# First three gate and up strips of an FFN summed tile by tile of x, with x loaded on a second DMA queue

## The chip, the cores and the metric

The kernel runs on one core of a Trainium2 chip. The metric is device time in microseconds (us) from one launch to its end. The kernel before was timed in three runs: 2579.68, 2580.84 and 2581.11 us, median 2580.84. Beside the timed runs there is one profiled execution, whose trace all rows below come from.

## What is computed

One decoder layer on 320 tokens (256 of a prompt, 64 of eight samples), model width 2048, feed-forward width 5632. The part that the change touches is the first feed-forward block and the norm ahead of it:

```python
def rmsnorm(x, g):
    y = xf * lax.rsqrt(jnp.mean(xf * xf, axis=-1, keepdims=True) + EPS)
    return (y * g.astype(jnp.float32)).astype(x.dtype)

def swiglu_ffn(x, wg, wu, wd):
    return (jax.nn.silu(x @ wg) * (x @ wu)) @ wd

def block(x, ...):
    x = x + FFN_RES * swiglu_ffn(rmsnorm(x, n_f1), f1_g, f1_u, f1_d)
    m, s_new, b_new = mixer(rmsnorm(x, n_mix), ...)
    x = x + m
    x = x + cross_attn(rmsnorm(x, n_xa), mk, mv, xa_q, xa_o)
    x = x + FFN_RES * swiglu_ffn(rmsnorm(x, n_f2), f2_g, f2_u, f2_d)
```

All of it is in float32.

## The kernel before, in words

The activations lie transposed: the model width is cut into 16 tiles of 128 rows (KT = 16), and each tile xs[k] holds 320 tokens as columns. A product of a 128x128 weight block with such a tile is written as three matmuls (mm3, lines 173 to 179): weights and activations are each split in a rounded high part and the rest, and high·high, high·low and low·high are summed in PSUM. Lines 176, 177 and 178 are these three, in this order.

Weights come in units of 128x1024 float32 (512 KB), that is eight 128x128 blocks. fetch (line 126) loads one into a raw buffer (three of them) from SP's DMA queue, ACT casts the high part (line 116) and DVE subtracts the low part (line 117), into four pairs of buffers. unit (line 137) keeps the fetches up to four units ahead of their use. A unit feeds 8 products, 24 matmuls.

ffn (line 232) computes the hidden width in parts of eight strips of 128. For each strip, strip (line 181) sums the gate over all 16 tiles of x into one PSUM accumulator, and then the up projection into the next; there are four such accumulators (tag acc, line 89) and four small ones (tag sm, line 92). The norm is applied behind the product: DVE multiplies the gate's sum by r, the reciprocal root mean square (line 242), ACT applies SiLU (243), DVE multiplies by r again (244) and by the up sum (249), and the result is split into high and low. The down products of the part follow, 16 tiles of eight products each.

r of the first block is made by first_root (line 269), which is called behind the first gate strip: ACT squares each x tile, POOL adds the squares up (line 212), a matmul with a matrix of ones sums over the partitions (219), and root (line 189) forms the power -1/2 by Ln, Exp and a Newton step: two table loads, four ACT instructions, two DVE instructions (lines 192 to 197).

At the start (lines 320 to 326) SP's queue is given: vec (the constants with the norms' gains), x tile 0, the first weight unit, x tiles 1 to 3 and 4 to 7, the second unit, x tiles 8 to 11 and 12 to 15; scaled_split (line 226) multiplies each tile by its gain from vec and splits it on ACT (228) and DVE (229). setup (line 275) holds small work on vec (lines 292 to 301) that is not needed before the mixer.

Every instruction stream is in order on its engine. The order in each stream is drawn up when the program is built: an instruction is taken by its priority, which is its place in the source unless the source raises it (as fetch does), among those that are ready by the builder's own reckoning.

Of the kernel before, what the change touches and what calls it, by code (L numbers as in the profile page):

```python
# [17 lines left out]
P = 128  # L18
# [16 lines left out]
MEM = 256  # L35
EPS = 1e-6
# [26 lines left out]
def hymba(tc, A, O):  # L63
# [15 lines left out]
    with (  # L79
# [15 lines left out]
        xgrp = [cp.tile([P, 4, T], F32, name=f"x{g}") for g in range(4)]  # L95
        xs = [xgrp[k // 4][:, k % 4, :] for k in range(KT)]
# [29 lines left out]
        def fetch(early=False):  # L126
            with contextlib.nullcontext() if early else tc.high_priority():
                raw = tl(mp, [P, 1024], F32, "raw", 3)
                g, u = divmod(fetched[0], 2)
                nc.sync.dma_start(raw, A["w"][g, :, u * 1024 : (u + 1) * 1024])  # L130
                hi = tl(mp, [P, 1024], F32R, "whi", 4)
                lo = tl(mp, [P, 1024], F32R, "wlo", 4)
                split(hi, lo, raw)
                units.append((hi, lo))
            fetched[0] += 1
# [52 lines left out]
        # r = (ps / n + eps) ** -0.5, the tables' value and one step of Newton's  # L188
# [37 lines left out]
        def scaled_split(k, name):  # L226
            h, l = pair("xg")
            nc.scalar.activation(h, xs[k], AF.Copy, scale=norm(name, k))  # L228
            nc.vector.scalar_tensor_tensor(l, xs[k], norm(name, k), h.bitcast(F32), ALU.mult, ALU.subtract)  # L229
            return h, l  # L230

        def ffn(pool, xg, root_of, done, setup=None):
            for pi, np_ in enumerate(PARTS):
                last_part = pi == len(PARTS) - 1
                hs = []
                for _ in range(np_):
                    pg = acc()
                    strip(xg, pg[:, :T])
                    if pi == 0 and not hs:
                        r = root_of()  # L240
                    t = tl(pool, [P, T], F32, "fa", 2)
                    nc.vector.tensor_tensor(t, pg[:, :T], r, ALU.mult)  # L242
                    nc.scalar.activation(t, t, AF.Silu)  # L243
                    nc.vector.tensor_tensor(t, t, r, ALU.mult)  # L244
                    pu = acc()
                    strip(xg, pu[:, :T])
                    hp = pair("h")
                    h = tl(pool, [P, T], F32, "fb", 2)
                    nc.vector.tensor_tensor(h, pu[:, :T], t, ALU.mult)  # L249
                    split(*hp, h)  # L250
                    hs.append(hp)
# [12 lines left out]

        # first FFN
# [3 lines left out]
        def first_root():  # L269
            stat = Stat()  # L270
            for k in range(KT):
                stat.add(xs[k])
            return stat.rstd()

        def setup(fp):
# [27 lines left out]
            # the memory's root mean square  # L303
# [31 lines left out]
            # a projection of the prompt's memory, tokens on the partitions  # L335
# [327 lines left out]
        # cross attention  # L663
# [151 lines left out]
        # second FFN  # L815
        with phase("ffn2") as fp:
# [11 lines left out]
            for k0, k1 in ((0, 1), (1, 4), (4, 8), (8, 12), (12, 16)):  # L828
                y = xgrp[k0 // 4][:, k0 % 4 : k0 % 4 + k1 - k0, :]
                nc.vector.tensor_tensor(y, y, r.unsqueeze(1).to_broadcast([P, k1 - k0, T]), ALU.mult)  # L830
                nc.sync.dma_start(O["y"][:, k0:k1, :], y)
# [20 lines left out]
def ffn_groups(w_gate, w_up, w_down):  # L852
    g, u, d = strips(w_gate), strips(w_up), downs(w_down)
    out = []
    f0 = 0
    for pi, np_ in enumerate(PARTS):
        for j in range(f0, f0 + np_):
            out += [g[j : j + 1], u[j : j + 1]]
        out.append(d[pi])
        f0 += np_  # L860
# [3 lines left out]
def pack(i):  # L864
    f = {k: np.asarray(v) for k, v in i.items()}
    groups = ffn_groups(f["ffn1_w_gate"][0], f["ffn1_w_up"][0], f["ffn1_w_down"][0])
# [20 lines left out]
    x = np.ascontiguousarray(x.T.reshape(KT, P, T).transpose(1, 0, 2))  # L887
# [90 lines left out]
```

## Time and profile before

| what | value |
|---|---|
| median of three runs | 2580.84 us (2579.68 to 2581.11) |
| span of the profiled execution | 2581.1 us |
| matmul instructions | 17280 |
| TensorE (PE) busy, share of the span | 2538.0 us, 98% |
| VectorE (DVE) busy | 1473.7 us, 57% |
| ScalarE (ACT) busy | 1076.9 us, 42% |
| GpSimd (POOL) busy | 100.1 us, 4% |
| bytes moved by DMA | 397.37 MB, mean 154 GB/s |

The profiled execution's span differs from the median by 0.3 us. PE is TensorE's matmuls, PEld its weight loads; SPq and ACTq are the sequencers of SyncE and ScalarE, which issue DMAs. A busy time is summed over instructions that can overlap in the pipeline, so what the matmuls cost is read from the distance between starts.

### The profile page before, as it was taken

How to read it: one execution, taken by the hardware profiler on the slowest of the kernel's cores; microseconds unless marked ns; L12 is line 12 of the kernel's file. 1: busy time of each engine (PE TensorE's matmuls, PEld its weight loads, DVE VectorE, ACT ScalarE, POOL GpSimd, SP SyncE). 2: the span in 40 equal slices, each digit the busy share in tenths (PEclk: the TensorE clock that was granted, in tenths of full speed). 3: DMA queues.
4: the chain of work that ended last, by engine and by line, in shares of the span. 5: the costliest groups of instructions: out<-in, count | busy, mean ns of one | idle time of the engine just before them, and what ended most of it. 6: DMA issues, size and time to landing. Idle time of an engine off the chain costs nothing.

```text
span 2581.1 us, 41685 instructions
## 1 busy us (share of the span) xinstructions
PE 2538.0 (98%) x17280; PEld 2491.3 (97%) x17280; DVE 1473.7 (57%) x2110; ACT 1076.9 (42%) x1487; POOL 100.1 (4%) x105
## 2 busy tenths in 40 slices
PE   7999999999999999999999999999999999999997
PEld 7999999999999989999998898999999999999997
DVE  6544444444444478788878775744444444444444
ACT  6333333333233354565655744532333333333334
POOL 4000000000000020000000020200000000000002
PEclk9999999999999999999999999999999999999999
DMA  7444444444444465444444554444444444444443
GB/s 234 156 151 150 148 150 152 148 150 152 148 149 153 148 195 160 146 156 141 150 144 146 198 176 150 147 152 148 150 152 148 150 152 148 150 153 148 150 152 107
DMA packets 111790, 397.37 MB, mean 154 GB/s; under 512 B 12656, under 2 KB 16368, under 8 KB 111600
## 3 DMA queue, kind: packets, MB, share of 16 engines
q1 hardware_dynamic: 111600, 394.70, 48.1%
q8 instruction: 136, 2.23, 0.3%
q14 instruction: 54, 0.44, 0.0%
HBM read 384.90 MB, written 9.76 MB: 153 GB/s over the span
## 4 chain that ended last, share of the span: by engine, by line
PE 92%; DVE 4%; ACT 2%; issue 1%; DMA 0%; POOL 0%; DVEq 0%; ACTq 0%; POOLq 0%
PE acc L176 29%; PE acc L177 29%; PE acc L178 29%; DVE wlo L117 1%; PE sm L512 1%; PE sm L605 1%; ACT whi L116 0%; DVE xgl L229 0%; DVE t L343 0%; PE sm L571 0%; ACT L194 0%; DVE hl L117 0%; ACT t L549 0%; DVE x L811 0%; PE sm L616 0%
## 5 line engine op out<-in xcount | busy, mean ns | idle before, releaser
L116 ACT CAST whi<-raw 128x1024 fp32r<-128x1024 f32 x688 | 721.7, 1049 | 1369.4 <-PE acc L177 983.7
L117 DVE TENSOR_TENSOR wlo<-raw,whi 128x1024 fp32r<-128x1024 f32 x688 | 849.6, 1235 | 557.2 <-ACT whi L116 556.7
L176 PE MATMUL acc<-xgh,whi 128*128 128x320 f32 x3648 | 1140.5, 313 | 11.5 <-ACT whi L116 9.4
L177 PE MATMUL acc<-xgl,whi 128*128 128x320 f32 x3648 | 1130.6, 310 | 3.5 <-DVE xgl L117 1.9
L178 PE MATMUL acc<-xgh,wlo 128*128 128x320 f32 x3648 | 1129.7, 310 | 1.8 <-DVE wlo L117 1.8
L176 PEld LDWEIGHTS acc<-xgh,whi 128*128 128x128 f32 x3648 | 686.8, 188 | 17.2 <-ACT whi L116 9.4
L177 PEld LDWEIGHTS acc<-xgl,whi 128*128 128x128 f32 x3648 | 687.2, 188 | 7.0 <-DVE xgl L229 3.2
L178 PEld LDWEIGHTS acc<-xgh,wlo 128*128 128x128 f32 x3648 | 686.7, 188 | 2.5 <-DVE wlo L117 2.5
L176 PE MATMUL acc<-hh,whi 128*128 128x320 f32 x1728 | 534.3, 310 | 2.4 <-DVE x L658 1.5
L178 PE MATMUL acc<-hh,wlo 128*128 128x320 f32 x1728 | 534.5, 309 | 0.0
L177 PE MATMUL acc<-hl,whi 128*128 128x320 f32 x1728 | 533.9, 309 | 0.0
L176 PEld LDWEIGHTS acc<-hh,whi 128*128 128x128 f32 x1728 | 324.1, 188 | 4.6 <-issue 3.0
L177 PEld LDWEIGHTS acc<-hl,whi 128*128 128x128 f32 x1728 | 324.3, 188 | 0.3 <-issue 0.2
L178 PEld LDWEIGHTS acc<-hh,wlo 128*128 128x128 f32 x1728 | 324.3, 188 | 0.2
L259 DVE SCALAR_TENSOR_TENSOR x<-acc,x 128x320 f32<-128x320 f32 x192 | 94.0, 491 | 223.0 <-PE acc L178 222.9
L212 POOL TENSOR_TENSOR ssq<-ssq,sq 128x320 f32<-128x320 f32 x74 | 83.8, 1133 | 1925.2 <-ACT sq L210 1021.0
L411 DVE SCALAR_TENSOR_TENSOR hl<-u,vec,hl 128x256 f32<-128x256 f32 x240 | 115.4, 481 | 2.3
L249 DVE TENSOR_TENSOR fb<-acc,fa 128x320 f32<-128x320 f32 x88 | 43.3, 492 | 111.0 <-PE acc L178 110.9
L242 DVE TENSOR_TENSOR fa<-acc,r 128x320 f32<-128x320 f32 x88 | 43.2, 492 | 109.1 <-PE acc L178 109.0
L229 DVE SCALAR_TENSOR_TENSOR xgl<-x,vec,xgh 128x320 fp32r<-128x320 f32 x48 | 47.3, 1016 | 0.9 <-ACT xgh L228 0.9
L117 DVE TENSOR_TENSOR hl<-fb,hh 128x320 fp32r<-128x320 f32 x88 | 43.2, 491 | 0.0
L244 DVE TENSOR_TENSOR fa<-fa,r 128x320 f32<-128x320 f32 x88 | 42.6, 485 | 0.6 <-ACT fa L243 0.6
(198 smaller groups left out, 1029.7 us busy)
## 6 DMA issues: line engine op xcount, KB each, us to landing
raw<-in_w SPq DMA_DIRECT2D x688, 512.0 KB, 3.8
t<-in_mem SPq DMA_DIRECT2D x8, 512.0 KB, 5.9
t<-in_s SPq DMA_DIRECT2D x8, 512.0 KB, 4.9
out_ss<-t SPq DMA_DIRECT2D x8, 512.0 KB, 3.6
kv<-in_ck SPq DMA_DIRECT2D x8, 512.0 KB, 6.3
kv<-in_cv SPq DMA_DIRECT2D x8, 512.0 KB, 6.2
t4k<-in_mem SPq DMA_DIRECT2D x4, 512.0 KB, 5.0
x<-in_x SPq DMA_DIRECT2D x3, 640.0 KB, 6.9
```

The lines of the kernel that those rows point to most:

```text
L116: nc.scalar.copy(hi, src)
L117: nc.vector.tensor_tensor(lo, src, hi.bitcast(F32), ALU.subtract)
L176: nc.tensor.matmul(out, hi, xh, start=first, stop=False)
L177: nc.tensor.matmul(out, hi, xl, start=False, stop=False)
L178: nc.tensor.matmul(out, lo, xh, start=False, stop=last)
L212: nc.gpsimd.tensor_tensor(self.total, self.total, s, ALU.add)
L229: nc.vector.scalar_tensor_tensor(l, xs[k], norm(name, k), h.bitcast(F32), ALU.mult, ALU.subtract)
L242: nc.vector.tensor_tensor(t, pg[:, :T], r, ALU.mult)
L244: nc.vector.tensor_tensor(t, t, r, ALU.mult)
L249: nc.vector.tensor_tensor(h, pu[:, :T], t, ALU.mult)
L259: nc.vector.scalar_tensor_tensor(xs[n], ps[:, :T], 0.5, xs[n], ALU.mult, ALU.add)
L411: nc.vector.scalar_tensor_tensor(dw[:, :NP], u[:, j : j + NP], cw, dw[:, :NP], ALU.mult, ALU.add)
```

## The change

x gets a layout of its own: the gains of the first norm stand as 16 columns ahead of the 16 tiles, so that one transfer brings the gains and tile 0 (x0). The x tiles are loaded in six pieces on ACT's DMA queue; SP's queue holds weights alone. The first weight unit is loaded and split in three pieces of 256, 512 and 256 columns. vec comes last on ACT's queue. Nine matmuls of ones by ones stand ahead of the first product. The first three strips' gate and up are summed together: for each tile of x, six products into six accumulators (four acc, two sm), then the next tile; the weights are packed in that order. r is computed behind all of these. gate and up are helpers that hold the lines 241 to 250 of before. At the end y goes out in six pieces instead of five.

```diff
+XCUTS = ((0, 1), (1, 2), (2, 4), (4, 8), (8, 12), (12, 16))
+HEAD = 3
...
-        xgrp = [cp.tile([P, 4, T], F32, name=f"x{g}") for g in range(4)]
-        xs = [xgrp[k // 4][:, k % 4, :] for k in range(KT)]
+        x0 = cp.tile([P, KT + T], F32, name="x0")
+        xparts = [x0[:, KT:].unsqueeze(1)]
+        for k0, k1 in XCUTS[1:]:
+            xparts.append(cp.tile([P, k1 - k0, T], F32, name=f"x{k0}"))
+        xs = [xp[:, k - k0, :] for (k0, k1), xp in zip(XCUTS, xparts) for k in range(k0, k1)]
...
-        def fetch(early=False):
+        def fetch(cuts=(0, 1024), early=False):
...
+                for a, b in zip(cuts, cuts[1:]):
+                    nc.sync.dma_start(raw[:, a:b], A["w"][g, :, u * 1024 + a : u * 1024 + b])
+                for a, b in zip(cuts, cuts[1:]):
+                    split(hi[:, a:b], lo[:, a:b], raw[:, a:b])
...
-        def ffn(pool, xg, root_of, done, setup=None):
+        def ffn(pool, xg, root_of, done, setup=None, head=None):
...
-                for _ in range(np_):
+                if pi == 0 and head is not None:
+                    r, strips_ = head(xg)
+                    for pg, pu in strips_:
+                        hs.append(up(pu, gate(pg, r)))
+                while len(hs) < np_:
                     pg = acc()
                     strip(xg, pg[:, :T])
...
-        def first_root():
+        def first_strips(xg):
             stat = Stat()
+            ps = [acc() for _ in range(4)] + [sm() for _ in range(2 * HEAD - 4)]
+            i = 0
             for k in range(KT):
+                xg.append(scaled_split(k, "ffn1", x0[:, k : k + 1]))
                 stat.add(xs[k])
-            return stat.rstd()
+                for p in ps:
+                    if i % 8 == 0:
+                        w = unit()
+                    mm3(p[:, :T], w, i % 8, *xg[k], k == 0, k == KT - 1)
+                    i += 1
+            return stat.rstd(), list(zip(ps[::2], ps[1::2]))
...
-            nc.sync.dma_start(vec, A["vec"])
-            xg = []
-            for k0, k1 in ((0, 1), (1, 4), (4, 8), (8, 12), (12, 16)):
-                nc.sync.dma_start(xgrp[k0 // 4][:, k0 % 4 : k0 % 4 + k1 - k0, :], A["x"][:, k0:k1, :])
-                if k0 in (0, 4):
-                    fetch(True)
-                xg += [scaled_split(k, "ffn1") for k in range(k0, k1)]
+            nc.scalar.dma_start(x0, A["x"][:, : KT + T])
+            fetch((0, 256, 768, 1024), True)
+            for (k0, k1), xp in zip(XCUTS[1:], xparts[1:]):
+                nc.scalar.dma_start(xp.rearrange("p a b -> p (a b)"), A["x"][:, KT + k0 * T : KT + k1 * T])
+            fetch(early=True)
+            nc.scalar.dma_start(vec, A["vec"])
+            warm = sm()
+            for _ in range(9):
+                nc.tensor.matmul(warm[:, :P], ones, ones, start=True, stop=True)
             stat1 = Stat()
-            ffn(fp, xg, first_root, lambda n: stat1.add(xs[n]), setup)
+            ffn(fp, [], None, lambda n: stat1.add(xs[n]), setup, first_strips)
```

## Rows read from the trace of the kernel before

**Rows 1.** The page: busy us, share of the span, instruction counts by engine.
```profile
PE 2538.0 (98%) x17280; PEld 2491.3 (97%) x17280; DVE 1473.7 (57%) x2110; ACT 1076.9 (42%) x1487; POOL 100.1 (4%) x105
```

**Rows 2.** Timeline at the first down product: start us, us, engine, line, out<-in.
```profile
132.26 0.31 PE L176 MATMUL acc<-xgh,whi 128*128 128x320 f32 x1
...
132.70 0.31 PE L176 MATMUL acc<-hh,whi 128*128 128x320 f32 x1
```

**Rows 3.** Timeline of PE at the start; brackets: idle before, who ended it.
```profile
9.39 0.63 PE L176 MATMUL acc<-xgh,whi 128*128 128x320 f32 x1 [9.39 <-ACT whi L116]
...
15.09 0.47 PE L176 MATMUL acc<-xgh,whi 128*128 128x320 f32 x1
15.35 0.37 PE L177 MATMUL acc<-xgl,whi 128*128 128x320 f32 x1
```

**Rows 4.** Waits of PE, 0 to 130 us: us in total, times, longest us.
```profile
PE acc L178 <- DVE wlo L117: 1.8, 2, 1.5
PE acc L176 <- ACT xgh L228: 1.4, 1, 1.4
```

**Rows 5.** Timeline of SP's queue at the start: DMA issues.
```profile
1.18 0.42 SPq L323 DMA_DIRECT2D x<-in_x  x1
1.65 0.42 SPq L130 DMA_DIRECT2D raw<-in_w  x1
...
20.24 0.42 SPq L323 DMA_DIRECT2D x<-in_x  x1
```

**Rows 6.** Windows from the start: length, PE, PEld, DVE, ACT, POOL, PEclk, DMA share, GB/s.
```profile
0.00:8.25 8.25, 0.00 (x0) 0.00 (x0) 0.96 (x4) 1.95 (x3) 1.04 (x8) 1.00 0.71 195
0.00:12.30 12.30, 2.55 (x8) 2.15 (x9) 3.60 (x9) 5.95 (x12) 1.83 (x9) 1.00 0.78 248
```

**Rows 7.** Timeline of ACT and DVE at the start.
```profile
0.73 1.28 ACT L295 ACT_TABLE_LOAD   x1 [0.73 <-PEq L954]
...
3.22 0.17 DVE L292 TENSOR_TENSOR lmax<-vec 128x8 f32<-128x8 f32 x1 [3.22 <-DMA vec<-in_vec]
...
3.74 0.55 ACT L228 ACTIVATE xgh<-x,vec 128x320 fp32r<-128x320 f32 x1
...
8.30 1.04 ACT L116 CAST whi<-raw 128x1024 fp32r<-128x1024 f32 x1 [4.01 <-DMA raw<-in_w]
...
9.37 1.23 DVE L117 TENSOR_TENSOR wlo<-raw,whi 128x1024 fp32r<-128x1024 f32 x1 [4.50 <-ACT whi L116]
```

**Rows 8.** Timeline at the second FFN's first root: from the ones matmul to the gate.
```profile
1641.26 0.70 PE L219 MATMUL sm<-ssq,ones 128*128 128x320 f32 x2
...
1641.31 1.05 ACT L116 CAST whi<-raw 128x1024 fp32r<-128x1024 f32 x1 [1.49 <-PE acc L177]
...
1642.38 1.28 ACT L192 ACT_TABLE_LOAD   x1
...
1644.64 1.28 ACT L194 ACT_TABLE_LOAD   x1
...
1647.97 0.49 DVE L242 TENSOR_TENSOR fa<-acc,r 128x320 f32<-128x320 f32 x1
```

**Rows 9.** Timeline at the kernel's end: last matmul, and y's pieces behind r.
```profile
2565.54 0.81 PE L221 MATMUL sm<-sq,ones 128*128 128x320 f32 x2
...
2570.67 5.77 DVE L830 TENSOR_TENSOR x<-x,r 128x320 f32<-128x320 f32 x5
```

**Rows 10.** Windows behind the last matmul; the granted clock is the third last column.
```profile
2566.40:2568.40 2.00, 0.00 (x0) 0.00 (x0) 0.00 (x0) 1.98 (x3) 0.00 (x0) 1.00 0.00 0
2568.40:2569.00 0.60, 0.00 (x0) 0.00 (x0) 0.00 (x0) 0.59 (x2) 0.00 (x0) 0.71 0.00 0
2569.00:2571.00 2.00, 0.00 (x0) 0.00 (x0) 1.31 (x3) 0.55 (x2) 0.00 (x0) 0.50 0.00 0
```

**Rows 11.** Timeline: last POOL step of the memory's square sum, and its ones matmul.
```profile
65.37 1.60 POOL L314 TENSOR_TENSOR mtot<-mtot 128x256 f32<-128x256 f32 x1
...
189.02 0.59 PE L316 MATMUL sm<-mtot,ones 128*128 128x256 f32 x2
```

More of the change, by code (lines that the diff above doesn't have):

```diff
@@ L124, in hymba @@
         upos = [0]
-        def fetch(early=False):
+        def fetch(cuts=(0, 1024), early=False):
             with contextlib.nullcontext() if early else tc.high_priority():
                 raw = tl(mp, [P, 1024], F32, "raw", 3)
-                g, u = divmod(fetched[0], 2)
-                nc.sync.dma_start(raw, A["w"][g, :, u * 1024 : (u + 1) * 1024])
                 hi = tl(mp, [P, 1024], F32R, "whi", 4)
                 lo = tl(mp, [P, 1024], F32R, "wlo", 4)
-                split(hi, lo, raw)
+                g, u = divmod(fetched[0], 2)
+                for a, b in zip(cuts, cuts[1:]):
+                    nc.sync.dma_start(raw[:, a:b], A["w"][g, :, u * 1024 + a : u * 1024 + b])
+                for a, b in zip(cuts, cuts[1:]):
+                    split(hi[:, a:b], lo[:, a:b], raw[:, a:b])
                 units.append((hi, lo))
@@ L224, in rstd, with scaled_split, gate, up @@
                 return r
-        def scaled_split(k, name):
+        def scaled_split(k, name, gain=None):
             h, l = pair("xg")
-            nc.scalar.activation(h, xs[k], AF.Copy, scale=norm(name, k))
-            nc.vector.scalar_tensor_tensor(l, xs[k], norm(name, k), h.bitcast(F32), ALU.mult, ALU.subtract)
+            gain = norm(name, k) if gain is None else gain
+            nc.scalar.activation(h, xs[k], AF.Copy, scale=gain)
+            nc.vector.scalar_tensor_tensor(l, xs[k], gain, h.bitcast(F32), ALU.mult, ALU.subtract)
             return h, l
-        def ffn(pool, xg, root_of, done, setup=None):
+        def ffn(pool, xg, root_of, done, setup=None, head=None):
+            def gate(pg, r):
+                t = tl(pool, [P, T], F32, "fa", 2)
+                nc.vector.tensor_tensor(t, pg[:, :T], r, ALU.mult)
+                nc.scalar.activation(t, t, AF.Silu)
+                nc.vector.tensor_tensor(t, t, r, ALU.mult)
+                return t
+            def up(pu, t):
+                hp = pair("h")
+                h = tl(pool, [P, T], F32, "fb", 2)
+                nc.vector.tensor_tensor(h, pu[:, :T], t, ALU.mult)
+                split(*hp, h)
+                return hp
             for pi, np_ in enumerate(PARTS):
@@ L240, in ffn @@
                         r = root_of()
[L241 to L244, printed above, removed]
+                    t = gate(pg, r)
                     pu = acc()
                     strip(xg, pu[:, :T])
[L247 to L251, printed above, removed]
+                    hs.append(up(pu, t))
                 w = None
@@ L827, in hymba @@
             r = stat1.rstd()
-            for k0, k1 in ((0, 1), (1, 4), (4, 8), (8, 12), (12, 16)):
-                y = xgrp[k0 // 4][:, k0 % 4 : k0 % 4 + k1 - k0, :]
+            for (k0, k1), y in zip(XCUTS, xparts):
                 nc.vector.tensor_tensor(y, y, r.unsqueeze(1).to_broadcast([P, k1 - k0, T]), ALU.mult)
@@ L849, in downs, with ffn_groups @@
     return out
-def ffn_groups(w_gate, w_up, w_down):
+def ffn_groups(w_gate, w_up, w_down, head=0):
     g, u, d = strips(w_gate), strips(w_up), downs(w_down)
     out = []
+    if head:
+        a = np.stack([w[j] for j in range(head) for w in (g, u)], axis=1)
+        a = a.reshape(P, 2 * head, KT, P).transpose(0, 2, 1, 3).reshape(P, -1, 2048)
+        out.append(a.transpose(1, 0, 2))
     f0 = 0
     for pi, np_ in enumerate(PARTS):
-        for j in range(f0, f0 + np_):
+        for j in range(max(f0, head), f0 + np_):
             out += [g[j : j + 1], u[j : j + 1]]
@@ L865, in pack @@
     f = {k: np.asarray(v) for k, v in i.items()}
-    groups = ffn_groups(f["ffn1_w_gate"][0], f["ffn1_w_up"][0], f["ffn1_w_down"][0])
+    groups = ffn_groups(f["ffn1_w_gate"][0], f["ffn1_w_up"][0], f["ffn1_w_down"][0], HEAD)
     def rows(w):
@@ L886, in pack @@
     x = np.concatenate([f["x_prompt"][0], f["x_sample"].reshape(NS, DM)], axis=0)
-    x = np.ascontiguousarray(x.T.reshape(KT, P, T).transpose(1, 0, 2))
+    x = x.T.reshape(KT, P, T).transpose(1, 0, 2).reshape(P, KT * T)
+    x = np.concatenate([f["norm_ffn1"].reshape(KT, P).T, x], axis=1)
     mem = np.ascontiguousarray(f["mem_prompt"][0].T.reshape(KT, P, MEM).transpose(1, 0, 2)).reshape(P, 4, 1024)
```

## The prediction

> **What bounds the kernel now.** I read the page's busy shares first: PE is busy for 98% of the span, every other engine for at most 57% [rows 1]. Then the distance between PE's starts in steady state: 132.26 to 132.70 is three matmuls, 0.147 us each for 320 columns, which is the 2.4 GHz level [rows 2]. From the first down product at 132.70 on, the work and its order stay as they are, but for the end. So the change is worth what it moves that one start. Ahead of it PE does 16 strips of 48 matmuls, 768 x 0.1467 = 112.6 us. The start therefore lies 132.7 - 112.6 = 20.1 us later than PE alone would need, and this loss is all that there is to win.
>
> Where it lies: PE's first product is at 9.39, behind the cast of the first weight unit [rows 3]; its DMA was issued at 1.65 and its cast began at 8.30 [rows 5, 7]. Then about 22 matmuls, up to 15.45, start 0.26 to 0.27 us apart, which is 320 columns at 1.2 GHz [rows 3]. (The granted column of the first windows reads 1.00 even so; I go by the spacing.) At the full rate 22 would have taken 3.2 us of these 6.1, so 2.9 are lost. The other 7.8 us are single waits and slowed splits: for a low part of weights, up to 1.5 us, for x tiles that SP issued as late as 20.24 since it stood on a raw buffer, 1.4 us, and smaller ones [rows 4, 5].
>
> **The change part by part: the start.** ACT issues seven DMAs. Before, none is issued there; on SP such an issue follows the one ahead by 0.47 us [rows 5]. 0.74 + 7 x 0.46 gives 4.0 us; a table load of 1.28 stands ahead of ACT's first real instruction, then the scaling of x0, 0.55, and the cast of the first weight piece [rows 7]. The cast is 256 columns; between 0.55 for 320 and 1.04 for 1024 I estimate 0.45. PE's first product then starts at 6.2 us. Low end 4.5, if the builder puts the first casts among the DMA issues (the first two transfers of before were used at 3.22 and 3.74, and two short ACT instructions follow [rows 7]). High end 7.8, if the nine matmuls of ones hold PE longer than I think: a pair of 320-column halves takes 0.70 at the full rate [rows 8], so nine pairs of 128 columns lie between 9 x 0.43 and 9 x 0.75 us, from 1.0 on. I take the low one, which hides them behind the load. They do count as activity: before, the spacing shortened 6.1 us after PE's first instruction [rows 3], so now at about 7.1, and only 0.5 us is lost to the low rate instead of 2.9.
>
> The next limit is the second weight unit. It is behind the first on SP's queue, 1.05 MB, while ACT's queue moves x. No run here shows two queues; I take it that they share the bytes evenly, so 2.1 MB must have moved. Before, 195 GB/s x 8.25 us = 1.6 MB had moved by 8.25 and 248 x 12.3 = 3.05 MB by 12.3 [rows 6], which puts 2.1 MB at 9.6 us. Transfers also end later than their turn: the first unit stood behind 0.36 MB and was used when 1.6 MB had moved, not 0.9 [rows 6, 7]. So it lands between 9.6 and 11.5; I take 10.2. Cast 1.04 and subtraction 1.23 [rows 7] make its low part ready at 12.5, and PE stands on the third product's matmul until then. 22 more matmuls end the unit at 15.7, where 48 would have needed 7.0: loss 8.7. Later units arrive every 3 us or so against 3.5 us of use; ACT and DVE stand in order on x tiles while they should split weights. I give this 1.1 us (0 to 3; before, such waits and slow splits came to several us [rows 4]). Loss up to the end of the head: 9.8, from 7.5 to 13. The Trainium skill says on the page "DMA: Bandwidth & Descriptors", section "Issuing engines are not separate DMA queues", that transfers interleave on the same engines whoever starts them, and that a second issuer saves issue time alone. That speaks against a gain from ACT's queue; no trace here has two queues. If weights had the whole rate for themselves, the unit would land some 2 us earlier, and the sum would be 2 us lower.
>
> Against this stand the waits for x, which go: a tile is needed only every 18 matmuls, 2.6 us, instead of every 0.44.
>
> **The end of the head.** All six sums end together, in the last 18 matmuls. The next strip needs one of the four large accumulators, and the first to come free is that of gate 0, once DVE has multiplied it by r. r is now computed behind the head: the ones matmul, two table loads, four ACT and two DVE instructions. Before, the first r was hidden behind strips 2 to 4, since their accumulators were free. Now PE has nothing else. The price is a row: in the second FFN the same chain starts with the ones matmul at 1641.26, just behind a weight unit's end; ACT first casts a freed unit (1641.31, 1.05), then loads a table at 1642.38 and one at 1644.64, and the gate's multiply starts at 1647.97 and takes 0.49 [rows 8]. That is 7.2 us from the ones matmul to the free accumulator. At the kernel's end, where no cast stands in the way, it is 2570.67 - 2565.54 + 0.49 = 5.6 us [rows 9]. The head ends on a weight unit's end, so I take 7.2 (5.6 to 7.4). Before, the small matmul cost about 1 us.
>
> Then the clock. PE stands for about 6.5 us behind the ones matmul. At the kernel's end the last matmul is over at 2566.35, and the granted clock falls from 1.00 to 0.50 within 2568.4 to 2569.0 [rows 10]. So PE would resume at 1.2 GHz and run so for at most the 6.1 us of the start, which lost 2.9 [rows 3]. I take 2.0 (0 to 3). The Trainium skill, "TensorE: Matmul & The Clock Gate", section "Why this matters for your kernels", has the same rule: a long idle gap of PE between bursts brings the clock back to half. The trace agrees at its end, where the clock halves within 2.7 us of the last matmul.
>
> The gating of three strips comes in one heap behind r: some 2 us of DVE each, by 0.49 us rows, hidden under the next strips' 7 us each, since the next accumulator is needed only 7 us later. y's sixth piece adds one DVE start and one issue, 0.15 us; vec's small work moves to later.
>
> **The sum.** Before 20.1. After 9.8 + 7.2 + 2.0 = 19.0. With 0.15 at the end that is -0.9 us against the profiled execution of 2581.1, which is 0.3 above the median; against the median of 2580.84 I get 2579.9. The ends: 7.5 + 5.6 + 0 = 13.1 (2574) and 13 + 7.4 + 3 = 23.4 (2584.5). So the start gives some 10 us and the wait for r takes nearly all of it back.
>
> **The rivals.** *r comes early.* If the builder puts the ones matmul into a gap of PE ahead of the head's end, r is ready and PE waits only for one multiply, about 0.7 us. Loss 9.8 + 0.7, time 2580.84 - 9.4 = 2571.4. For it: the squares are done some 20 us ahead of the head's end. Against it: the same case later, where the memory's square sum is complete at 67.0 and its ones matmul runs at 189.02, at its place in the source [rows 11]. Matmuls that are ready and stand earlier go first. Chance 0.14.
>
> *DVE stands on vec (slower).* The small work on vec is DVE's first instruction before, at 3.22 [rows 7]. Now vec is last on ACT's queue, behind 2.6 MB of x; at an even share it lands when some 5 MB have moved, at 18 to 20 us by the rate of [rows 6]. If the builder reckons it earlier and puts that work among the first splits, DVE stands from some 10 us on, with the low parts of weights behind it, and PE stops when the first two units are used, about 15 at best. It resumes at about 21.5: 6 to 10 us more, 2580 + 8 = 2588. It costs as soon as vec lands later than DVE's turn by more than the one unit that PE has in hand, 3.5 us. For it: ACT stood 4.01 us on the first cast, so the order was drawn for an earlier landing [rows 7]. Against it: x tiles 12 to 15 land just ahead of vec, so a builder that counts bytes puts it behind them. Chance 0.10.
>
> *Everything as forecast, but the clock holds.* Then 2578; it is inside the range.
>
> **How the numbers follow.** Forecast 0.76, centre 2579.9, own range 2574 to 2584.5; early r 0.14 at 2571.4; vec 0.10 at 2588. A measurement of this kernel can tell about 0.2%, 5.2 us. Faster by more: 0.12 of early r and 0.10 of the forecast, 0.22. Slower by more: 0.09 of vec and 0.02 of the forecast, 0.11. The range takes in early r and the forecast's bounds, 2570.5 to 2585.
>
> **What would show it.** First real product near 6 us; the second unit's low part near 12.5; the first down product near 131.6 instead of 132.7. One gap of PE of about 6.5 us behind the ones matmul near 52, a cast and two table loads in it, and 0.267 us spacing behind it. It is wrong if the ones matmul runs well ahead of the 288th product's matmul, if that gap is under 3 us, or if DVE's first vec instruction waits for DMA while weights are unsplit.

## The result, and the profile after

The changed kernel takes 2591.97 us, median of four runs (2590.73 to 2592.56); the kernel before, run beside it, 2580.26 us (2579.01 to 2581.11). The ratio is 1.0046, with a 95% interval of 1.0034 to 1.0058. I had predicted 2579.9 and a range up to 2585. The span of the profiled execution is 2590.8 us against 2581.1. Of all the timed runs below one is left out of the ratios: one of e11's ten took 3532.17 us at a mean granted clock of 0.654.

The page's busy shares tell nothing new: PE has 2539.6 us (98%) with the 18 instructions of the ones matmuls added to [rows 1]. The loss lies ahead of the first down product, which now starts at 146.18 us; before it was 132.70 [rows 2].

PE at the start of the changed kernel (timeline; start us, us, engine, line, operation, out<-in; in brackets the idle time before it and who ended it):

```profile
0.99 3.64 PE L356 MATMUL sm<-ones 128*128 128x128 f32 x18 [0.99 <-POOL ones L285]
19.10 1.17 PE L183 MATMUL acc<-xgh,whi 128*128 128x320 f32 x3 [14.47 <-ACT xgh L236]
...
24.45 0.31 PE L183 MATMUL acc<-xgh,whi 128*128 128x320 f32 x1
```

The first product comes at 19.10; before it was 9.39 [rows 3]. The bracket names x0's scaled tile, not a weight. Up to 24.45 starts are 0.27 us apart, the 1.2 GHz level. ACT's stream shows why (same columns; ACTq is its DMA issuing):

```profile
0.73 0.41 ACTq L348 DMA_DIRECT2D x<-in_x  x1
1.17 1.42 ACTq L351 DMA_DIRECT2D x<-in_x  x3
2.62 1.28 ACT L121 ACT_TABLE_LOAD   x1 [2.62 <-issue]
...
6.99 0.41 ACT L121 CAST whi<-raw 128x256 fp32r<-128x256 f32 x1 [0.32 <-DMA raw<-in_w]
7.00 3.67 ACTq L351 DMA_DIRECT2D x<-in_x  x2
10.71 1.04 ACT L121 CAST whi<-raw 128x1024 fp32r<-128x1024 f32 x1 [3.31 <-DMA x<-in_x]
12.02 1.04 ACT L121 CAST whi<-raw 128x1024 fp32r<-128x1024 f32 x1 [0.26 <-DMA raw<-in_w]
17.54 1.04 ACT L121 CAST whi<-raw 128x1024 fp32r<-128x1024 f32 x1 [4.47 <-DMA raw<-in_w]
17.54 0.33 ACTq L353 DMA_DIRECT2D vec<-in_vec  x1
18.49 0.56 ACT L236 ACTIVATE xgh<-x 128x320 fp32r<-128x320 f32 x1
```

x0 was issued at 0.73. The first unit's last piece is cast at 6.99. But x0's scaling (18.49) stands in the stream behind everything listed: two more DMA issues that hold ACT's sequencer for 3.67 us, the casts of units 2, 3 and 4, and vec's issue. The last issue waits there for a semaphore that the transfer of x tiles 4 to 7 still holds (in the trace the issues of both queues take eight semaphores in turn). Unit 4's cast waits 4.47 us for its DMA, issued at 10.22. Before, the scaling of x tile 0 was ACT's third instruction, at 3.74 [rows 7].

The bytes that PE needs first were not late: x0 landed 4.3 us behind its issue, at 5.0. The windows of the start and of the stretch behind the head (start, length, busy PE, PEld, DVE, ACT, POOL, then granted clock, DMA share, GB/s):

```profile
5.00:10.00 5.00, 0.00 (x0) 0.00 (x0) 1.54 (x3) 1.29 (x3) 0.00 (x0) 0.73 1.03 406
10.00:15.00 5.00, 0.00 (x0) 0.00 (x0) 0.17 (x1) 2.09 (x2) 0.00 (x0) 0.50 1.04 395
...
70.00:75.00 5.00, 2.45 (x9) 2.01 (x8) 1.87 (x4) 4.90 (x8) 0.00 (x0) 0.50 0.20 66
```

DMA moves 406 and 395 GB/s from 5 to 15 us (before: 351 and 312), while PE does nothing and ACT and DVE are busy for 3.4 and 1.7 of these 10 us. The clock fell to 0.50 before PE had its first product, so the ones matmuls, over at 4.63, were for nothing (e4 tests it).

The other wait, behind the head (timelines of PE, then of ACT and DVE):

```profile
64.05 0.70 PE L226 MATMUL sm<-ssq,ones 128*128 128x320 f32 x2
69.25 1.19 PE L344 MATMUL sm<-mtot,ones 128*128 128x256 f32 x2 [4.49 <-ACT sq L200]
72.99 0.64 PE L183 MATMUL acc<-xgh,whi 128*128 128x320 f32 x1 [2.55 <-DVE fa L243]
```
```profile
64.15 1.04 ACT L121 CAST whi<-raw 128x1024 fp32r<-128x1024 f32 x1 [2.21 <-PE sm L184]
65.80 1.04 ACT L121 CAST whi<-raw 128x1024 fp32r<-128x1024 f32 x1 [0.60 <-DMA raw<-in_w]
66.86 1.28 ACT L199 ACT_TABLE_LOAD   x1
...
69.12 1.28 ACT L201 ACT_TABLE_LOAD   x1
```

The ones matmul is at 64.05, PE's next strip at 72.99: 8.94 us. Two casts stand ahead of the first table load, where the chain of [rows 8] had one; the second waits 0.60 us for its DMA. Behind it the starts are 0.267 us apart until 79.0.

So the accounts of the 112.6 us of matmuls close: head end 64.05 - 288 x 0.1467 = 21.8 us lost, wait 8.94, low clock behind it 146.18 - 72.99 - 480 x 0.1467 = 2.8. The sum is 33.5 against the 20.1 of before: 13.4 us, as the first down product shows.

### The profile page after: what moved, and what is told of

It reads as the page before. It is cut to its first block, busy times and chain, and to the rows that moved or that the text cites. A ratio compares the mean times of both kernels' runs of the same rounds, so it can differ in the third digit from the quotient of the medians.

```text
span 2590.8 us, 41731 instructions
## 1 busy us (share of the span) xinstructions
PE 2539.6 (98%) x17298; PEld 2493.2 (96%) x17298; DVE 1477.3 (57%) x2113; ACT 1075.9 (42%) x1488; POOL 97.5 (4%) x105
## 4 chain that ended last, share of the span: by engine, by line
PE 91%; DVE 4%; ACT 2%; DMA 2%; issue 1%; SPq 0%; POOL 0%; DVEq 0%; ACTq 0%; POOLq 0%
PE acc L183 29%; PE acc L184 29%; PE acc L185 29%; DVE wlo L122 2%; DMA raw<-in_w 1%; PE sm L542 1%; DVE xgl L237 1%; ACT whi L121 1%; PE sm L635 1%; PE sm L601 0%; DVE t L373 0%; ACT L201 0%; DVE hl L122 0%; ACT t L579 0%; DMA t<-in_mem 0%
## 5 line engine op out<-in xcount | busy, mean ns | idle before, releaser
L121 ACT CAST whi<-raw 128x1024 fp32r<-128x1024 f32 (+1 forms) x690 | 722.0, 1047 | 1379.6 <-PE acc L184 981.4
L122 DVE TENSOR_TENSOR wlo<-raw,whi 128x1024 fp32r<-128x1024 f32 (+1 forms) x690 | 848.1, 1230 | 559.8 <-ACT whi L121 559.2
L217 ACT ACTIVATE sq<-x 128x320 f32<-128x320 f32 x75 | 34.6, 463 | 15.2 <-DVE x L278 12.9
```

The lines of the kernel that those rows point to most:

```text
L121: nc.scalar.copy(hi, src)
L122: nc.vector.tensor_tensor(lo, src, hi.bitcast(F32), ALU.subtract)
L217: nc.scalar.activation(s, x, AF.Square)
```

## The experiments

"First" is PE's first product, "down" the first down product, both from the profiled execution; the ratio is to runs of the kernel before on the same chip.

| kernel | median us | ratio, 95% interval | first | down |
|---|---|---|---|---|
| before | 2580.0 to 2581.3 | 1 | 9.39 | 132.70 |
| changed | 2591.97 | 1.0046 (1.0034 to 1.0058) | 19.10 | 146.18 |
| e1b x0 first | 2591.55 | 1.0041 (1.0026 to 1.0056) | 6.19 | 144.63 |
| e2 x on SP | 2587.25 | 1.0024 (1.0015 to 1.0033) | 4.85 | 140.56 |
| e3 r early | 2584.83 | 1.0014 (1.0005 to 1.0023) | 19.12 | 136.26 |
| e4 no ones matmuls | 2592.30 | 1.0044 (1.0027 to 1.0060) | 19.37 | 146.17 |
| e6 x on SP, r early | 2584.59 | 1.0012 (1.0003 to 1.0021) | 4.85 | 137.81 |
| e7 order of need, r early | 2568.48 | 0.9958 (0.9944 to 0.9973) | 4.85 | 121.07 |
| e7 again | 2569.66 | 0.9955 (0.9941 to 0.9969) | 4.85 | 122.44 |
| e9 order of need, r late | 2580.62 | 1.0004 (0.9994 to 1.0013) | 4.85 | 133.97 |
| e10 e7 without ones matmuls | 2577.55 | 0.9984 (0.9975 to 0.9993) | 4.04 | 130.78 |
| e11 e7, tiles 0 to 3 on ACT | 2577.61 | 0.9989 (0.9980 to 0.9998) | 7.98 | 130.44 |
| e12 e10, squarings on POOL | 2573.62 | 0.9976 (0.9965 to 0.9987) | 4.09 | 124.09 |
| e14 e6, squarings on POOL | 2581.99 | 1.0006 (0.9997 to 1.0015) | 4.85 | 133.16 |
| e15 changed, squarings on POOL | 2602.16 | 1.0085 (1.0069 to 1.0102) | 19.11 | 155.37 |
| p1 before, x on ACT | 2594.55 | 1.0056 (1.0039 to 1.0073) | 8.22 | 148.19 |
| p2 before, first unit in pieces | 2580.72 | 0.9998 (0.9989 to 1.0008) | 8.24 | 131.86 |

**The late start: ACT's stream or the queues?** Two kernels tell it. e1b raises x0's scaling alone:

```diff
-                xg.append(scaled_split(k, "ffn1", x0[:, k : k + 1]))
+                with tc.high_priority() if k < 1 else contextlib.nullcontext():
+                    xg.append(scaled_split(k, "ffn1", x0[:, k : k + 1]))
```

> Edit: the scaling of x's tile 0 alone gets the builder's high priority, so that on ACT it stands ahead of the first weight casts; both queues stay. Theory O (order: what starts late is ACT's in-order stream, in which x0's scaling, at 18.49 us, stands behind two DMA issues that take 3.67 us, the casts of units 2 to 4 and vec's issue): PE's first real product comes at 5.5 to 7 us instead of 19.1, but x1's scaling still stands where x0's stood, so PE stands again after 18 matmuls; the first down product moves from 146.2 to 142 to 145, the time from 2592.0 to 2588 to 2591. Rival Q (queues: with two queues x0 and the first weights land late, and the order only hides it): the first product stays at 12 us or later, the time stays within 1 us of 2592. Rival S (the six-way sum itself is slow): first product early, and the first down product stays at 146.

The first product came at 6.19, then PE stood 10.6 us for x1's scaling, which now had x0's place, and resumed at 19.76: theory O, and Q falls, since x0 was scaled at 5.29 and the first unit's last piece cast at 7.24 with both queues at work. The first down product came 1.55 us earlier, as expected; the time moved by 0.4 us, within its uncertainty and less than the 1 to 4 us expected.

e2 takes the issues off ACT:

```diff
-            nc.scalar.dma_start(x0, A["x"][:, : KT + T])
+            nc.sync.dma_start(x0, A["x"][:, : KT + T])
...
-                nc.scalar.dma_start(xp.rearrange("p a b -> p (a b)"), A["x"][:, KT + k0 * T : KT + k1 * T])
+                nc.sync.dma_start(xp.rearrange("p a b -> p (a b)"), A["x"][:, KT + k0 * T : KT + k1 * T])
...
-            nc.scalar.dma_start(vec, A["vec"])
+            nc.sync.dma_start(vec, A["vec"])
```

> Edit: x's six DMAs and vec's go back to SP's queue; the sums in six accumulators, the three pieces, the warm matmuls and the place of vec stay. Theory O (ACT's in-order stream is what starts late): without DMA issues on ACT, x0's scaling stands ahead of the casts of units 2 to 4; first real product at 5.5 to 7 us instead of 19.1; the wait for r behind the head stays 8 to 9 us with some 3 us of low clock behind it; the first down product at 134 to 138 instead of 146.2, the time 2580 to 2584. Rival Q (the transfers of x and weights are slow on any queue, since 16 engines are shared): first product at 12 us or later, time 2588 or more. Rival S (the six-way sum is slow by itself): the first product is early, but PE stands within the head, and the time stays above 2588.

The first product came at 4.85, earlier than expected, but the first down product only at 140.56 and the time at 2587.25: 3 us more than expected. SP's queue and ACT in e2 (timelines) show what I had missed:

```profile
4.98 3.06 SPq L138 DMA_DIRECT2D raw<-in_w  x3
...
8.78 0.56 ACT L236 ACTIVATE xgh<-x,x 128x320 fp32r<-128x320 f32 x1 [0.66 <-DMA x<-in_x]
...
17.24 0.55 ACT L236 ACTIVATE xgh<-x,x 128x320 fp32r<-128x320 f32 x1
17.69 1.03 ACT L121 CAST whi<-raw 128x1024 fp32r<-128x1024 f32 x1
```

Now ten x tiles' scalings and squarings stand between unit 1's casts and unit 2's (17.69), and PE stood 8.9 us, from 9.87 to 18.77, for it. Two orders are behind that. On SP's queue unit 2 stands behind all of x: issued at 4.98, it landed 9.9 us later, at 14.9, so with its cast of 1.03 PE would have stood some 6 us in any case. The other 3 us are ACT's stream. Neither Q nor S came out as stated, since the first product was early and the time below 2588; but PE did wait for a transfer, late by its place in the queue.

e4 asks what the ones matmuls bring to the changed kernel.

> Edit: the nine matmuls of ones ahead of the first product are left out; nothing else. In the changed kernel the granted clock had fallen back to 0.50 by 10 us, 9 us ahead of the first real product at 19.1. Theory: the nine matmuls bring nothing there, so the time stays within 1 us of 2592 and the half-rate spacing still lasts for some 5 us behind the first product. Rival: they still bring part of the clock forward; then the half rate lasts 1 us or more longer than in the changed kernel and the time rises by 0.5 to 2 us.

Nothing: 2592.30 against 2591.97, first down product 146.17.

**The wait for r.** e3 writes the squares of tiles 13 to 15 and the root ahead of tile 12's products:

```diff
-                stat.add(xs[k])
+                if k <= 12:
+                    stat.add(xs[k])
+                if k == 12:
+                    for kk in range(k + 1, KT):
+                        stat.add(xs[kk])
+                    rr.append(stat.rstd())
```

> Edit: the squares of x's tiles 13 to 15 and the root of their sum are written ahead of the products of tile 12, so the ones matmul stands 72 matmuls ahead of the head's end; the start stays as in the changed kernel. Theory R (r computed behind the head costs 8.9 us of PE standing and some 2.8 us of half rate behind it): the first product stays at 19.1, the gap of 8.9 us behind the ones matmul goes, PE waits under 1.5 us for the first multiply; the first down product at 134 to 137 instead of 146.2, time 2580 to 2583. Rival: the gap only moves, since ACT and DVE are behind with splits of weights at that point (two table loads and six instructions put ahead of casts): PE then stands 4 us or more for a cast or a low part, the time 2586 or more.

The first down product moved by 9.9 us to 136.26, inside what was expected; PE waited 0.99 us for the first multiply and the clock stayed at 1.00. The median, 2584.83, is 7.1 us lower than the changed kernel's, not 9.9, and above the 2580 to 2583 expected; the section on the hardware shows a scatter of that size, but not that it is the reason here.

**Do the two add?** e6 has the edits of e2 and e3 together.

> Edit: both of the earlier ones at once: x's and vec's DMAs on SP's queue, and the root of the squares written ahead of the products of tile 12. Alone, the first took the first down product from 146.18 to 140.56 us, the second to 136.26. Theory (two separate losses, the late start and the wait for r, that add): first down product at 146.2 - 5.6 - 9.9 = 130.7, 129.5 to 132; time 2576 to 2580. Rival (the same ACT time is behind both, so that removing one removes part of the other): first down product at 133 to 136, time 2580 to 2584.

They do not: the first down product is at 137.81, later than with r early alone and later than the rival had it too. The wait of 8.7 us for unit 2 is as in e2, and the wait for r is there again, 4.6 us. DVE in e6 (timeline):

```profile
58.74 0.49 DVE L203 SCALAR_TENSOR_TENSOR sm<-sq,sm 128x320 f32<-128x320 f32 x1 [2.64 <-ACT sm L202]
59.27 0.49 DVE L204 SCALAR_TENSOR_TENSOR r<-sm,r 128x320 f32<-128x320 f32 x1
59.71 4.48 DVE L122 TENSOR_TENSOR wlo<-raw,whi 128x1024 fp32r<-128x1024 f32 x2
64.12 0.88 DVE L243 TENSOR_TENSOR fa<-acc,r 128x320 f32<-128x320 f32 x2
```

r is ready at 59.76, and the multiply stands behind two subtractions of weights.

**Everything in order of need.** e7 puts all on SP's queue in the order in which PE needs it, with r early as in e3:

```diff
-            nc.scalar.dma_start(x0, A["x"][:, : KT + T])
+            nc.sync.dma_start(x0, A["x"][:, : KT + T])
             fetch((0, 256, 768, 1024), True)
-            for (k0, k1), xp in zip(XCUTS[1:], xparts[1:]):
-                nc.scalar.dma_start(xp.rearrange("p a b -> p (a b)"), A["x"][:, KT + k0 * T : KT + k1 * T])
+            part(1)
             fetch(early=True)
+            part(2)
+            fetch(early=True)
+            part(3)
+            part(4)
+            part(5)
-            nc.scalar.dma_start(vec, A["vec"])
+            nc.sync.dma_start(vec, A["vec"])
```

(part(j) issues piece j of x on SP's queue.)

> Edit: as the kernel with x on SP and r early, and SP issues in the order in which PE needs things: x tile 0, the first weight unit in three pieces, tile 1, unit 2, tiles 2 and 3, unit 3, then the rest of x and vec last. In the kernel with x on SP, unit 2's cast stood on ACT behind the scaling of nine x tiles, from 9.7 to 18.77 us; here it stands behind tile 1's. Theory O (what made the start late is order on in-order streams, not the speed of the transfers): first product at 4.8 to 5.5, unit 2 cast by 10 to 12, no wait of PE over 3 us in the head, no wait for r over 1.5 us; the head's 288 products end at 49 to 52, the first down product at 122 to 127 against 132.7 of the kernel before; time 2569 to 2576, faster than both kernels. Rival Q (the transfers bind: 2.6 MB of x and the units 2 to 6 have to pass within the first 25 us): PE stands for 4 us or more on raw weights or x in the head, the first down product at 128 to 133, the time 2576 to 2582.

> The kernel with the queue in order of need and r early once more, unchanged, as the partner of the runs beside it. Expected: 2568 to 2572, as before.

It takes 2568.48 and 2569.66 us, 0.42% and 0.45% less than before: faster than both kernels. PE's waits up to 150 us (line waited for: us in total, times, longest):

```profile
PE sm L370 <- POOL ones L285: 1.0, 1, 1.0
PE acc L183 <- ACT whi L121: 0.6, 1, 0.6
PE acc L185 <- DVE wlo L122: 0.3, 1, 0.3
```

The loss ahead of the first down product is 121.07 - 112.6 = 8.5 us, of which 4.85 is the start. So the sums tile by tile do what they can, once the streams are in order.

e9 has the root behind the head again.

> Edit: the kernel with the queue in order of need, but with the root behind the head, where the changed kernel has it. It prices the wait for r when the start is good. Theory R: PE stands 8 to 9.5 us between the ones matmul and the first multiply's end, and the half rate behind it costs some 2.8 us more, as in the changed kernel (8.94 us; 22 matmuls 0.267 us apart): first down product 10 to 12 us behind that of the kernel with r early, the time higher by as much, 2580 to 2587. Rival: with the start in order, splits run ahead and no cast stands in the chain of r: 5.6 to 7 us and a time 7 to 9 us above that with r early.

The time is 11 to 12 us above e7's, the first down product 12.9 us later, a little more than expected. PE stood 10.0 us for the multiply and ran at the low rate behind it, which is 2.7 us more (133.97 - 60.89 - 480 x 0.1467). Here it is the memory's squarings of setup that stand in the chain, two of them ahead of its first table load (at 50.40 and 51.86) and one within it (ACT, timeline, lines 339 and 199 to 202):

```profile
57.42 0.47 ACT L201 ACTIVATE r<-r 128x320 f32<-128x320 f32 x1
57.80 1.04 ACT L339 ACTIVATE t4k<-t4k 128x1024 f32<-128x1024 f32 x1
58.74 0.42 ACT L202 ACTIVATE sm<-r 128x320 f32<-128x320 f32 x1
```

**A second queue as such.** e11 is e7 with x0 and tiles 1 to 3 issued by ACT.

> Edit: the kernel with the queue in order of need and r early, but x's tiles 0 to 3 are issued by ACT, three issues ahead of all its other work; SP has the weights, and the other tiles in their order. Theory O (a second queue as such costs and brings little; what cost was work of ACT behind issues and waits): first product at 5 to 7 us, second unit's cast within 1.5 us of 9.45, first down product within 2 us of 121.07, time within 2 us of that kernel. Rival Q (two queues slow the transfers that PE needs first): PE stands 3 us or more for unit 2 or 3, the time 3 us or more higher.

The first product is at 7.98 and the time 8 to 9 us higher than e7's, which misses theory O's 2 us. But the transfers were not what PE stood for: it waited 2.8 us for x0's scaling, which the builder now put behind the first unit's casts (ACT at 7.37), and 4.8 us for the multiply by r. At the head's end 1.7 us of the late start are left (52.38 against 50.67); the multiply, with 2.7 us of low clock behind it, makes up the rest of the 9.4 us that the first down product lost. That wait e10 below has too, with one queue, so that the second queue led to it is not shown. The Trainium skill says on the page "DMA: Bandwidth & Descriptors", section "Issuing engines are not separate DMA queues", that a second issuer saves issue time alone; the runs agree: none of the three kernels with x on ACT's queue (changed, e11, p1) is faster than its partner with x on SP's (e2, e7, before).

p1 is the kernel before with only vec and x issued by ACT.

> Edit: the kernel before, with one part of the change alone: vec's and x's DMAs are issued by ACT; sums, pieces and all else as before. Theory O: the issues stand in ACT's stream, the first four ahead of its first table load, the last two (tiles 8 to 11 and 12 to 15) behind scalings and casts of the first tiles, so that x lands later than before and PE's first strip waits for it: first product within 1.5 us of before's 9.39, the first down product 2 to 8 us later than 132.70, time 2583 to 2589. Rival Q' (a queue of its own brings x faster, as the change would have it): the first down product 1 to 4 us earlier, time 2577 to 2580.

2594.55, outside both ranges of time and slower than the whole change. The first product is even earlier (8.22). But x's last two pieces are issued at 12.18 and 20.42 only, between casts, so the squares end late: PE stood 8.0 us for POOL's last sum ahead of the ones matmul at 50.68 and 5.1 us for the multiply, and its clock fell to 0.50.

p2 is the kernel before with only the first unit in pieces.

> Edit: the kernel before, with one part of the change alone: the first weight unit's DMA and split in three pieces of 256, 512 and 256 columns. There the cast of the whole unit began at 8.30 and PE at 9.39. Theory: the first piece lands some 3 us earlier, PE starts at 6 to 7.5, but then waits for x tiles and for later pieces, which land as before; the first down product 0.5 to 2.5 us earlier than 132.70, time 2578 to 2580.5. Rival: x's tiles set the pace of the first strip, and the early start is given back whole: first down product within 0.5 us of 132.70.

First product at 8.24, later than expected, where the bracket names x's scaling; first down product 0.84 us earlier, as the theory had it, and the time is the same within 0.1%.

**What the ones matmuls bring, and why r early fails.** e10 is e7 without them.

> Edit: the kernel with the queue in order of need and r early, without the nine matmuls of ones. There the first product comes at 4.85 and the half rate ends about 6.9 us; only some 6 products run at it. Theory W (the nine matmuls bring the full clock forward when work follows at once): without them the half rate lasts from 4.85 to about 11 us, some 15 to 22 products more are 0.12 us slower each, but PE waits for units 1 and 2 in that stretch in any case (0.6 and 0.3 us): first down product 1 to 2.5 us later than 121.07, the time higher by as much. Rival: PE waits for weights in that stretch anyway, so the time moves by less than 0.7 us.

The time is 8 to 9 us higher, far from both. The head itself ends only 0.7 us later (51.39 against 50.67), which is what the ones matmuls give: without them the first product comes 0.8 us earlier (4.04), but the starts stay 0.27 us apart up to 12.4. The rest is a wait of 6.0 us for the multiply by r, and the low clock behind it. The multiply has moved back by one place in DVE's order (DVE in e10, then in e7, timelines):

```profile
48.93 0.49 DVE L204 SCALAR_TENSOR_TENSOR r<-sm,r 128x320 f32<-128x320 f32 x1
52.52 1.23 DVE L122 TENSOR_TENSOR wlo<-raw,whi 128x1024 fp32r<-128x1024 f32 x1 [3.10 <-ACT whi L121]
54.41 2.62 DVE L122 TENSOR_TENSOR wlo<-raw,whi 128x1024 fp32r<-128x1024 f32 x1 [0.67 <-ACT whi L121]
56.95 0.87 DVE L243 TENSOR_TENSOR fa<-acc,r 128x320 f32<-128x320 f32 x2
```
```profile
47.54 1.22 DVE L122 TENSOR_TENSOR wlo<-raw,whi 128x1024 fp32r<-128x1024 f32 x1
48.67 0.48 DVE L243 TENSOR_TENSOR fa<-acc,r 128x320 f32<-128x320 f32 x1
52.33 1.22 DVE L122 TENSOR_TENSOR wlo<-raw,whi 128x1024 fp32r<-128x1024 f32 x1 [3.18 <-ACT whi L121]
```

In e7 the multiply stands behind one subtraction, whose cast ACT did at 45.12, ahead of the memory's squarings; in e10 it stands behind two, whose casts come behind them. The first squaring in turn waits for its DMA (ACT in e10):

```profile
50.49 1.06 ACT L343 ACTIVATE mtot<-t4k 128x1024 f32<-128x1024 f32 x1 [2.93 <-DMA t4k<-in_mem]
51.46 1.03 ACT L121 CAST whi<-raw 128x1024 fp32r<-128x1024 f32 x1
```

Three kernels take the memory's squarings out of ACT's stream:

```diff
-                    nc.scalar.activation(mtot, m, AF.Square)
+                    nc.gpsimd.tensor_tensor(mtot, m, m, ALU.mult)
...
-                    nc.scalar.activation(m, m, AF.Square)
+                    nc.gpsimd.tensor_tensor(m, m, m, ALU.mult)
```

> Edit: the kernel with the queue in order of need and r early but without the matmuls of ones (which took 2577.6 against 2568.5 to 2569.7), with the four squarings of the memory on POOL instead of ACT. There r was ready at 49.42, but DVE's multiply by it stood behind two subtractions of weight units until 56.95, which waited for ACT's casts, and these for the memory's squarings, which waited for their DMA (ACT at 50.49 behind 2.93 us of waiting). Theory M (the wait moved into ACT's stream by the memory's squarings): PE's wait for the first multiply falls from 6.0 us to under 2.5 and the half rate behind it goes; first down product at 123 to 126 instead of 130.78, time 2570 to 2574. Rival W (the lost warm-up is what costs): the wait is not the point; time stays at 2576 to 2578.

As theory M has it: the wait is 0.2 us, the first down product at 124.09, the time 2573.62. The multiply stands behind the same two subtractions as in e10, so what cost was that their casts were late, not the place as such. The time is still 4 to 5 us above e7's; the first down product shows 1.7 to 3.0 of it.

> Edit: the kernel with x on SP's queue and r early (2584.59; first down product at 137.81, where adding the two single gains gave 130.7), with the memory's squarings on POOL instead of ACT. Theory M: PE's wait of 4.6 us for the first multiply and the half rate behind it were the memory's squarings in ACT's stream ahead of the casts; first down product at 130 to 133, time 2576 to 2580. Rival: the splits of weights that stand ahead of the multiply on DVE are late for another reason (weights land late since x's DMAs hold SP's queue); the wait stays over 3 us, time 2582 to 2585.

Half of it: the wait falls from 4.6 to 2.3 us and the first down product to 133.16; the time, 2581.99, lies between the two. DVE's multiply still stands behind a subtraction, and its cast waited 4.01 us for the weights' DMA (ACT at 59.68), which is the rival's reason.

> Edit: the changed kernel, with the memory's four squarings on POOL instead of ACT; the start and the place of the root stay. In the changed kernel the chain from the ones matmul (64.05) to the first multiply's end took 8.94 us, with two casts in it. Theory M: the memory's work is not in that chain here, so the wait stays 7 to 9 us; time 2590 to 2592. Rival: with ACT freed of four squarings the second cast is done ahead of the ones matmul: the wait falls to 5.6 to 7 us, time 2587 to 2589.5.

Both wrong on the time: 2602.16, 10 us slower. The chain of r is 7.25 us (75.34 to 82.59), inside theory M's 7 to 9, with one cast in it:

```profile
75.40 1.04 ACT L121 CAST whi<-raw 128x1024 fp32r<-128x1024 f32 x1 [2.47 <-PE sm L184]
```

The second cast is gone from it, as the rival had it, and that is worth 1.7 us. But the head ends at 75.34 instead of 64.05, since DVE's splits slowed down beside POOL (last section). PE stood 5.7 us in two waits for low parts of weights of the large accumulators and 2.6 us in one of a small one, where the changed kernel had no such wait.

## Why the prediction was wrong

**What bounds the kernel** held: 112.6 us of matmuls ahead of the first down product, and 33.5 - 20.1 us of loss against before account for the change of it.

**The start** is the step that failed: "PE's first product then starts at 6.2 us". It came at 19.10. I had worked out when x0, the first piece and ACT's first two instructions would be done, and all of that was about right (first cast at 4.87, x0 there by about 5). What I did not ask is in which order the builder would put ACT's instructions: I took x0's scaling to be ACT's first real instruction, and asked for the builder's order only as a gain, for the low end. fetch raises its casts, the early fetch stands ahead of the head in the source, and x0's scaling had moved from the loads into the head, behind both. All that I needed stood in the diff: the line with scaled_split moved. The high end, 7.8, bounded the ones matmuls, not the order. That is 14.47 us of PE's waiting; in e1b, where that scaling alone is moved ahead, the first product is at 6.19, and in e2 and e7, with x on SP's queue, at 4.85. That 6.19 meets the 6.2 is luck: I had all seven issues ahead of ACT's work, and four stood there; x0's landing set its scaling, at 5.29.

**The second unit's low part** (12.5 predicted) was never the limit, though the unit's landing was sized well: 8.0 us behind its issue at 2.12, at 10.1 for 10.2. In e7, where it was the limit, its cast began at 9.45 and PE waited 0.6 and 0.3 us. The loss of the head, 9.8 predicted, is 8.4 there (50.67 - 42.25); this kernel lost 21.8. The kernel that I had summed up, streams in order and r late, is e9, which took 2580.62 for 2579.9. That is near in part by luck: its head lost 7.9 us for 9.8, its wait for r was 10.7 for 7.2, its low clock 2.7 for 2.0. Of the start of before I had read about 22 matmuls at the low rate; the rows have 20, up to 15.35, and a wait of 0.36 us among them, which changes no term by more than 0.3 us.

**The wait for r** was right as a mechanism: nothing else for PE, a gap, a cast and two table loads in it. Its size was off: 8.94 against 7.2 (high end 7.4), by the second cast of 1.04 and its wait of 0.60. e9 had 10.7 with the memory's squarings in it; e15, with one cast as in my row, 7.25. The row that I took it from has no setup beside it.

**The clock** was 2.8 for 2.0, inside its bounds.

**The rivals.** r did not come early: the ones matmul stood at its place in the source, behind the head, 25 us after the squares' sum was complete (38.6). But the row that I argued from does not make a rule: the memory's ones matmul, at its place in the source before (189.02), ran at 69.25 in the changed kernel, in the wait for r. DVE did not stand on vec: its first instruction on it ran at 25.03 without a wait. But DVE stood 6.98 us on a constant of setup (a mask) from 7.9 to 14.8, ahead of unit 2's subtraction; had x's first tiles been scaled in time, that would have been the next wait, which no run here shows by itself. The end was as predicted: y in six pieces of 5.83 us against five of 5.77.

**At the end of the span** only 9.7 of the 13.5 us are left; of the 3.8 us that went, 2.5 are the clock in the mixer, told below.

## What to carry to other kernels

Here ACT issued DMAs in its one stream, and an issue that had to wait for a semaphore (3.67 us) and a cast that waited for bytes (4.47 us) held back work whose inputs had long arrived. When a diff moves a line, list the new order of every in-order stream it touches before any duration is summed, and ask of the first thing that the critical engine needs what now stands ahead of it. A chain that the critical engine waits for (here r) has to be written early and kept clear on every engine that it passes; in e10 its last multiply stood behind two splits of weights that came late, and the time was 8 to 9 us above e7's.

## What the runs showed of the hardware

**The clock falls, or does not, in the same stretch of code.** From the first down product to the mixer's first ones matmul each of the profiled executions takes 825.7 to 826.4 us. The next 444 us are the same code too, and PE is partly idle there for some 4 us ahead of a second projection. Windows of that place (columns as above), in the kernel before and then in the changed one:

```profile
980.00:982.00 2.00, 0.61 (x3) 0.19 (x1) 2.00 (x5) 0.94 (x3) 0.00 (x0) 0.86 0.84 256
982.00:984.00 2.00, 1.94 (x7) 1.94 (x8) 1.48 (x5) 1.22 (x2) 0.00 (x0) 0.50 0.92 307
```
```profile
993.00:995.00 2.00, 0.87 (x5) 0.38 (x3) 2.00 (x4) 1.20 (x3) 0.00 (x0) 1.00 0.77 233
995.00:997.00 2.00, 1.67 (x11) 1.67 (x12) 1.70 (x5) 1.18 (x2) 0.00 (x0) 1.00 1.00 375
```

In before the clock halves, in the changed kernel it stays up, with the same work on either side. From that ones matmul to one and the same matmul 444 us on (sm<-qk), 13 of the 17 profiled executions take 443.7 us, before 446.2, e7 446.1 and 444.9, e14 444.8. So the execution of before that I compared with had 2.5 us of low clock there; most of the rest of the 3.8 us lies behind that matmul, where nearly the same code takes from 1173.4 to 1177.8 us. This is a scatter of single executions, as e7's two show, and it is in the spans of the kernel before, too: 2576.6 us at a mean clock of 0.997, 2583.7 at 0.994. What decides it in one execution no run here shows; a sum made against one trace is uncertain by it.

**POOL slows DVE.** In e15 POOL squares the memory while DVE splits x; in the changed kernel, otherwise the same, POOL only adds there (rows of the groups by line, up to 75 us: operation, count, then busy us and mean ns of one; e15, then the changed kernel):

```profile
L237 DVE SCALAR_TENSOR_TENSOR xgl<-x,x,xgh 128x320 fp32r<-128x320 f32 x15 | 21.9, 1497 | 0.0
```
```profile
L237 DVE SCALAR_TENSOR_TENSOR xgl<-x,x,xgh 128x320 fp32r<-128x320 f32 x15 | 16.0, 1103 | 0.0
```

A single one with POOL at rest takes 0.55 us. The Trainium skill, "SBUF — State Buffer", section "SBUF: two separate sides", says that DVE and GpSimd share one pair of ports, that whoever holds it has it for a whole instruction, and that DVE instructions with two inputs in SBUF need it against a GpSimd one that reads SBUF. The rows agree with it, 0.55 us by itself and 1.5 us in the mean beside POOL's squarings of 2.1 us each, though no row names the port as what DVE waits for.
